# Both affine passes of the inner normalizations on VectorE, in pieces of 512 columns

## Chip, cores and metric

The kernel runs on one core of one Trainium2 chip. The metric is device time in microseconds (us) of one execution, the median of three runs. An engine here is one of the five instruction streams of the core: TensorE (PE, matmuls; PEld its weight loads), VectorE (DVE), ScalarE (ACT), GpSimd (POOL) and SyncE (SP, which issues the transfers). Each executes its own instructions in order and waits on semaphores for the others.

## What is computed

A two-layer decoder trunk on 512 tokens of width 1024. Layer 0 has a sparse attention (compressed, selected and windowed keys) beside an attention into 256 memory rows; layer 1 has a block-sparse attention beside another memory attention. Each layer ends in a gated convolutional feed-forward of width 2816. Behind each attention and each feed-forward stands a residual sum with a layer normalization, so there are four:

```python
def layer_norm(x, g, b):
    mu = xf.mean(-1, keepdims=True)
    var = jnp.square(xf - mu).mean(-1, keepdims=True)
    return (xf - mu) * lax.rsqrt(var + LN_EPS) * g + b
...
        mix = jnp.concatenate([o_main, o_mem], axis=-1) @ w_out
        x = layer_norm(ALPHA * x + mix, ln1_g[layer], ln1_b[layer])
        ffn = conv_ffn(x, ...)
        x = layer_norm(ALPHA * x + ffn, ln2_g[layer], ln2_b[layer])
```

## The kernel before

The tokens lie in four tiles of 128 rows, `nat`, each 128x1024 in float32 (in the program nat_129 or nat_2_129 is tile 0, up to nat_132 or nat_5_132 for tile 3). Every matmul of the projections is done in three products of a high and a low half (`mm3`, line 120): ScalarE copies a value to its high half (`hi`, line 114), and VectorE or GpSimd subtracts to get the low half (`lo`, line 117; for weights, line 145). Weights come in pieces of 256 KB through five buffers `raw`, always issued by SyncE.

The stream runs: layer 0 attention (heads 0 to 11), output projection, normalization (place A below), feed-forward, normalization (place B), layer 1 values, projections and attention, output projection, normalization (place C), feed-forward, and the last normalization, which writes the output. The first three are done by `norm_xT` for each tile, 12 in all: `affine` normalizes the tile in place, and `to_xT` transposes it on TensorE (line 128, 2 x 4 transposes into `psPT`, three PSUM buffers) into `xh` and `xl`, the halves that all later projections read. The last normalization is `norm_out`, with cuts of its own (`OUT_CUT`).

`affine(tb, gt, bt, cut)` does the work of one tile. `stats` takes mean and variance on VectorE (lines 521, 522). Columns below `cut` are done on VectorE: line 553 computes (x - mu) * g in one instruction, line 560 computes x * y + b in pieces of at most 512. Columns from `cut` on are done by ScalarE and GpSimd: line 549 negates the mean (VectorE), line 550 subtracts it (ScalarE), line 551 multiplies by g (GpSimd), line 562 multiplies by y (ScalarE), line 563 adds b (GpSimd). Between the two passes `rstd` (lines 529 to 537) works out y, the reciprocal deviation, on VectorE in eleven instructions on one column each, by an integer guess and two refining steps. In `norm_xT` the cut is MID_CUT = 640, so VectorE has 640 columns (a second pass of 512 + 128) and GpSimd 384.

Around A and C, `tail_heads` does the last four heads of the attention, first for tokens 0 to 255 and then for 256 to 511, with the output projection of tiles 0 and 1 between (`out_part`: lines 498, 499 split the attention result, line 505 adds the product to `nat`), then the normalization of tiles 0 and 1, then projection and normalization of tiles 2 and 3. Line 280 writes a head's sum to `o`, which the projection reads. The feed-forward behind it starts with two column blocks done for tokens 0 to 255 first (96 matmuls of 128x256), which need only tiles 0 and 1. Around B, the feed-forward's last chunks are accumulated tile by tile (line 655 adds the product to `nat`), and the memory projections and the values of layer 1 (24 matmuls of 128x256 for each tile of tokens) follow.

The order in each engine's queue isn't that of the code. The framework's scheduler places the instructions by its own estimate of times, with a high priority for what stands under `high_priority(URGENT)`, as `norm_xT` and the sums of the heads do. What an edit changes in durations can therefore move other instructions.

Of the kernel before, what the change touches and what calls it, by code (L numbers as in the profile page):

```python
# [14 lines left out]
ALU = mybir.AluOpType  # L15
# [43 lines left out]
YB = (("PT", "PT"), ("mm", "mm"), ("S", "S"), ("PT", "O"))  # L59
HALVES = ((0, 512), (512, D))  # L60
OUT_CUT = ((0, 0), (0, 0), (512, 1024), (512, 768))
MID_CUT = 640
URGENT = 1000


class Trunk:
# [115 lines left out]
        self.xh = self.al("xh", R).rearrange("p (k t) -> p k t", k=KC)  # L182
        self.xl = self.al("xl", R).rearrange("p (k t) -> p k t", k=KC)

    # ---------------------------------------------------------------- setup
    def setup(self):
        nc, a = self.nc, self.a
        self.oh = self.al("kj")
        self.rb = self.one.tile([33, NH], F, name="rb")
        nc.vector.memset(self.rb[32:33, :], -BIG)  # L190
        self.nat = [self.al("nat") for _ in range(NT)]
        x = lambda tb, c0, c1: nc.sync.dma_start(self.nat[tb][:, c0:c1], a["x"][0, tb * 128:tb * 128 + 128, c0:c1])
        x(0, 0, 512)
        x(0, 512, D)
        nc.sync.dma_start(self.rb[0:32, :], a["rel_bias"])
        nc.sync.dma_start(self.oh[0:33, 0:NREV], a["onehot"])
        self.wkv = self.al("kj")
        nc.sync.dma_start(self.wkv.rearrange("p (k m) -> p k m", k=KC),
                          a["a_w_in"][0][:, 768:896].rearrange("(k p) m -> p k m", p=128))
        for tb in range(1, NT):  # L200
            x(tb, 0, D)
        self.ident = self.one.tile([128, 128], F, name="ident")
        make_identity(nc, self.ident)
        self.i2 = self.one.tile([64, 32], F, name="i2")
        nc.vector.tensor_add(self.i2, self.ident[0:64, 0:32], self.ident[0:64, 32:64])
        self.cw = self.one.tile([128, 2, NF * 3], F, name="cw")
        self.cb = self.one.tile([128, 2, NF], F, name="cb")
        self.new_xT()
        for tb in range(NT):
            self.to_xT(tb)  # L210
# [29 lines left out]
            self.nc.sync.dma_start(t[p:p + REP, c0:512], src)  # L240
        return t

    # ---------------------------------------------------------------- pieces of attention
    def q2(self, ps, half):
        t = self.al("qq", R)
        o, e = 64 * half, 64 - 64 * half
        self.nc.scalar.activation(t[o:o + 64, :], ps[o:o + 64, :], AF.Copy, scale=SC)
        self.nc.vector.scalar_tensor_tensor(t[e:e + 64, :], ps[o:o + 64, :], SC, t[o:o + 64, :].bitcast(F),  # L248
                                            op0=ALU.mult, op1=ALU.subtract)
        return t  # L250
# [69 lines left out]
                self.mm(o, v(c), ph[:, e0:e1], start and c == 0, False)  # L320
                self.mm(o, v(c), pl[:, e0:e1], False, last)

    # ---------------------------------------------------------------- memory attention
    def mem_kv(self, w, tag="mm", rt="kj"):
        nc, a = self.nc, self.a
        t = self.al("o", R)
# [74 lines left out]
    def new_o(self):  # L401
        self.o = self.al("o").rearrange("p (k t) -> p k t", k=KC)

    # ---------------------------------------------------------------- compressed keys and values
    def stacked(self, ps, row):
        t = self.al("p")
        self.hi(t[0:64, 0:S], ps[row:row + 64, :])
        self.hi(t[64:128, 0:S - 1], ps[row:row + 64, 1:S])
        return t
# [77 lines left out]
        self.lo(pl, ps, ph)  # L487
        return ph, pl

    # ---------------------------------------------------------------- projection back, norm  # L490
    def out_part(self, w, chunks, tb, first, last):
        nc = self.nc
        n = len(chunks)
        t = self.al("kj", R)[:, 0:256 * n].rearrange("p (s k t) -> p s k t", s=2, k=n)
        for k0 in range(0, n, 2):
            c = chunks[k0]
            src = self.o[:, c:c + 2, 128 * tb:128 * tb + 128]
            self.hi(t[:, 0, k0:k0 + 2, :], src)
            self.nc.gpsimd.tensor_sub(t[:, 1, k0:k0 + 2, :], src, t[:, 0, k0:k0 + 2, :].bitcast(F))
        for half in range(2):  # L500
            sl = slice(512 * half, 512 * half + 512)
            ps = self.ps("S" if last and tb % 2 else "mm")
            for k in range(n):
                self.mm3(ps, t[:, 0, k, :], t[:, 1, k, :], w[k][0][:, sl], w[k][1][:, sl], k == 0, k == n - 1)
            nc.vector.scalar_tensor_tensor(self.nat[tb][:, sl], self.nat[tb][:, sl], ALPHA if first else 1.0, ps,  # L505
                                           op0=ALU.mult, op1=ALU.add)
            if not last and (n > 2 or half):
                yield
# [31 lines left out]
    def affine(self, tb, gt, bt, cut, cut2=None, done=None):  # L540
        nc = self.nc
        x = self.nat[tb]
        cut2 = cut if cut2 is None else cut2
        with self.tc.high_priority(URGENT):
            mu, var = self.stats(tb)
        d, p = slice(0, cut), slice(cut, D)
        if cut < D:
            nm = self.small(1)
            nc.vector.tensor_scalar(nm, mu, -1.0, None, op0=ALU.mult)
            nc.scalar.activation(x[:, p], x[:, p], AF.Identity, bias=nm)  # L550
            nc.gpsimd.tensor_mul(x[:, p], x[:, p], gt[:, p])  # L551
        if cut:
            nc.vector.scalar_tensor_tensor(x[:, d], x[:, d], mu, gt[:, d], op0=ALU.subtract, op1=ALU.mult)  # L553
        with self.tc.high_priority(URGENT):
            y = self.rstd(var)
        for c0, c1, eng in ((0, cut2, nc.vector), (cut2, D, nc.gpsimd)):
            for c in range(c0, c1, 512):
                c = slice(c, min(c + 512, c1))
                if eng is nc.vector:
                    eng.scalar_tensor_tensor(x[:, c], x[:, c], y, bt[:, c], op0=ALU.mult, op1=ALU.add)  # L560
                else:
                    nc.scalar.activation(x[:, c], x[:, c], AF.Copy, scale=y)
                    eng.tensor_add(x[:, c], x[:, c], bt[:, c])
                if done:
                    done(c)
# [5 lines left out]
    def norm_xT(self, tb, gt, bt):  # L571
        with self.tc.high_priority(URGENT):
            self.affine(tb, gt, bt, MID_CUT)
            self.to_xT(tb)

    # ---------------------------------------------------------------- feed-forward
    def ffn(self, l, last):
        nc, a = self.nc, self.a
        self.los = (nc.gpsimd,)
# [99 lines left out]
            if tb < 2:  # L679
                yield  # L680

    # ---------------------------------------------------------------- layers
    def layer0(self):
        nc, a = self.nc, self.a
        w = a["a_w_in"][0]
# [233 lines left out]
```

## Time and profile before

| | us |
|---|---|
| median of 3 runs (1282.27 to 1283.21) | 1282.38 |
| span of the profiled execution | 1278.2 |
| median less that span | 4.2 |

The profile is of one execution; its span goes from the first to the last instruction, and a time of its own from outside isn't given. Busy time is counted by engine; a matmul's end is modelled, since matmuls overlap. The granted clock is the share of TensorE's full speed of 2.4 GHz (1.00 in most stretches; 0.50 is 1.2 GHz). In square brackets stands how long an engine was idle before an instruction, and whose end it waited for.

### The profile page before, as it was taken

Reading aid. Unit: us, or ns where it says so; the run is one execution under the profiler, and the core shown is the slowest. Engines: PE = TensorE matmul, PEld = TensorE weight load, DVE = VectorE, ACT = ScalarE, POOL = GpSimd, SP = SyncE. Lnnn points to the kernel's source line nnn. Section 1 sums busy time; section 2 is a strip of 40 time slices with the busy share of each in tenths; the row PEclk is TensorE's granted clock in tenths of the full one; section 3 lists DMA queues with packets and bytes.
Section 4 is the critical chain, followed back from the end, with each engine's and each line's share of the span. In section 5 each row is a group of like instructions: output and inputs, shape, how many; then the busy total and the mean of one; then the engine's idle time right before and its main releaser. Section 6 shows DMA issues by size and latency. Waiting matters only on the chain.

```text
span 1278.2 us, 18386 instructions
## 1 busy us (share of the span) xinstructions
PE 1231.1 (96%) x6400; PEld 1048.4 (82%) x6400; DVE 726.7 (57%) x1605; ACT 596.5 (47%) x1271; POOL 275.7 (22%) x364
## 2 busy tenths in 40 slices
PE   7899999989999999999998999998999999999996
PEld 6788888879888888888888898886988888888885
DVE  5457787898544444433385665558854444443347
ACT  6457776664433333333344877465443333332232
POOL 0146443543000000000053445344400000000004
PEclk9899999999999999999999999999999999999999
DMA  9772112242433333333414223234143333333321
GB/s 230 218 201 75 42 34 58 48 127 83 120 95 99 99 99 99 98 89 95 131 42 124 67 78 89 74 100 140 35 131 99 99 92 93 97 99 99 99 74 66
DMA packets 164724, 125.94 MB, mean 99 GB/s; under 512 B 10743, under 2 KB 141175, under 8 KB 164632
## 3 DMA queue, kind: packets, MB, share of 16 engines
q1 hardware_dynamic: 164632, 124.77, 34.0%
q8 instruction: 51, 0.84, 0.3%
q14 instruction: 41, 0.34, 0.1%
HBM read 121.65 MB, written 3.08 MB: 98 GB/s over the span
## 4 chain that ended last, share of the span: by engine, by line
PE 82%; DVE 10%; DMA 3%; ACT 2%; issue 1%; POOL 0%; SPq 0%; DVEq 0%; ACTq 0%; POOLq 0%
PE psmm L120 40%; PE psS L120 27%; PE psPT L120 7%; PE psO L120 5%; PE psPT L128 3%; DVE pt L117 1%; DMA kj<-in_mem_dram 1%; DVE st L521 1%; DVE p L295 1%; DVE nat L553 1%; DVE nat L560 1%; DVE nat L505 1%; ACT p L300 1%; DVE xl L117 1%; ACT pt L114 1%
## 5 line engine op out<-in xcount | busy, mean ns | idle before, releaser
L114 ACT ACTIVATE hi<-raw 128x512 fp32r<-128x512 f32 x370 | 213.5, 622 | 274.2 <-PE psS L120 181.3
L145 DVE TENSOR_TENSOR lo<-raw,hi 128x512 fp32r<-128x512 f32 x294 | 192.0, 692 | 188.6 <-ACT hi L114 187.1
L120 PE MATMUL psmm<-xh,hi 128*128 128x512 f32 (+1 forms) x560 | 212.1, 379 | 0.0
L120 PE MATMUL psmm<-xh,lo 128*128 128x512 f32 (+1 forms) x560 | 211.9, 378 | 0.0
L120 PE MATMUL psmm<-xl,hi 128*128 128x512 f32 (+1 forms) x560 | 211.8, 378 | 0.0
L145 POOL TENSOR_TENSOR lo<-raw,hi 128x512 fp32r<-128x512 f32 x76 | 99.3, 1330 | 399.8 <-ACT hi L114 398.3
L120 PE MATMUL psS<-xh,hi 128*128 128x512 f32 (+1 forms) x408 | 151.3, 371 | 0.9 <-ACT G L750 0.9
L120 PE MATMUL psS<-xl,hi 128*128 128x512 f32 (+1 forms) x408 | 151.5, 371 | 0.1
L120 PE MATMUL psS<-xh,lo 128*128 128x512 f32 (+1 forms) x408 | 150.9, 370 | 0.0
L120 PE MATMUL psmm<-hi,kj 128*128 128x512 f32 x392 | 137.3, 400 | 4.2 <-ACT kj L114 3.2
L120 PEld LDWEIGHTS psmm<-xh,lo 128*128 128x128 f32 x560 | 105.5, 188 | 18.9
L120 PEld LDWEIGHTS psmm<-xh,hi 128*128 128x128 f32 x560 | 105.4, 188 | 18.8 <-DVE qq L248 0.2
L120 PEld LDWEIGHTS psmm<-xl,hi 128*128 128x128 f32 x560 | 105.3, 188 | 18.8
L551 POOL TENSOR_TENSOR nat<-nat,p 128x384 f32<-128x384 f32 (+2 forms) x16 | 20.5, 1283 | 360.9 <-issue 329.5
L304 POOL TENSOR_SCALAR p<-p,s 128x128 f32<-128x128 f32 (+3 forms) x144 | 74.7, 536 | 96.4 <-DVE s L271 49.1
L300 ACT ACTIVATE p<-p,s 128x128 f32<-128x128 f32 (+3 forms) x144 | 79.9, 556 | 33.0 <-DVE s L295 32.2
L120 PEld LDWEIGHTS psmm<-hi,kj 128*128 128x128 f32 x392 | 73.7, 189 | 19.4 <-ACT kj L114 3.5
L120 PEld LDWEIGHTS psS<-xh,hi 128*128 128x128 f32 x408 | 77.5, 190 | 14.0 <-ACT G L750 1.0
L120 PEld LDWEIGHTS psS<-xl,hi 128*128 128x128 f32 x408 | 77.4, 190 | 13.3 <-DVE xl L117 0.3
L120 PEld LDWEIGHTS psS<-xh,lo 128*128 128x128 f32 x408 | 77.4, 190 | 12.8
L120 PE MATMUL psPT<-hi,kj 128*128 128x512 f32 x228 | 81.7, 389 | 0.0
L295 DVE CUSTOM_DVE_ANT_0 p<-psS,T 128x128 f32<-128x128 f32 (+3 forms) x144 | 66.1, 484 | 23.1 <-PE psS L120 19.9
(269 smaller groups left out, 2235.6 us busy)
## 6 DMA issues: line engine op xcount, KB each, us to landing
raw<-in_ffn_w_in_dram SPq DMA_DIRECT2D x176, 256.0 KB, 3.1
raw<-in_ffn_w_out_dram SPq DMA_DIRECT2D x88, 256.0 KB, 3.0
T<-bias_rows SPq DMA_DIRECT2D x144, 64.0 KB, 2.0
raw<-in_shared_w_kv_dram SPq DMA_DIRECT2D x24, 256.0 KB, 3.0
raw<-in_a_w_out_dram SPq DMA_DIRECT2D x16, 256.0 KB, 2.9
raw<-in_b_w_in_dram SPq DMA_DIRECT2D x16, 256.0 KB, 3.1
raw<-in_b_w_out_dram SPq DMA_DIRECT2D x16, 256.0 KB, 3.2
raw<-in_a_w_in_dram SPq DMA_DIRECT2D x14, 256.0 KB, 3.9
```

What stands on the lines that cost most here:

```text
L114: self.nc.scalar.activation(dst, src, AF.Copy)
L117: self.nc.vector.tensor_sub(dst, src, hi.bitcast(F))
L120: self.nc.tensor.matmul(o, l, r, start=start, stop=stop)
L128: self.nc.tensor.transpose(o, i, self.ident)
L145: eng.tensor_sub(l[:, c], raw, h[:, c].bitcast(F))
L295: nc.vector.tensor_tensor_reduce(L[i], dst[i], T[:, 384 - 128 * i:512], op0=ALU.add, op1=ALU.min, scale=1.0, scalar=BIG, accum_out=nm[:, i ...
L300: nc.scalar.activation(L[i], L[i], AF.Exp, bias=nm[:, i:i + 1], scale=-1.0, accum_out=sm[:, i:i + 1])
L304: nc.gpsimd.tensor_scalar(L[i], L[i], r[:, i - qs[0]:i - qs[0] + 1], 1.0, op0=ALU.mult, op1=ALU.mult)
L505: nc.vector.scalar_tensor_tensor(self.nat[tb][:, sl], self.nat[tb][:, sl], ALPHA if first else 1.0, ps, op0=ALU.mult, op1=ALU.add)
L521: nc.vector.bn_stats(st[:, 6 * j:6 * j + 6], x[:, c0:c1])
L551: nc.gpsimd.tensor_mul(x[:, p], x[:, p], gt[:, p])
L553: nc.vector.scalar_tensor_tensor(x[:, d], x[:, d], mu, gt[:, d], op0=ALU.subtract, op1=ALU.mult)
```

## The change

MID_CUT becomes 1024, so `norm_xT` gives all 1024 columns to VectorE and lines 549 to 551, 562 and 563 aren't reached for these twelve tiles. The first pass on VectorE, one instruction so far, is done in pieces of 512, as the second was. The last normalization has cuts of its own and keeps its instructions (its VectorE part of 512 columns is one piece).

```diff
-MID_CUT = 640
+MID_CUT = 1024
...
         if cut:
-            nc.vector.scalar_tensor_tensor(x[:, d], x[:, d], mu, gt[:, d], op0=ALU.subtract, op1=ALU.mult)
+            for c in range(0, cut, 512):
+                c = slice(c, min(c + 512, cut))
+                nc.vector.scalar_tensor_tensor(x[:, c], x[:, c], mu, gt[:, c], op0=ALU.subtract, op1=ALU.mult)
```

In the built program the scheduler moves other instructions too, at A, B and C; the transfers keep their order. In the changed kernel the first pass is line 555 and the second line 562. Two places follow.

VectorE's queue in place A, before, around the sum of the last head (line 280, into `o`) and tile 1's second pass (line 560):

```order
L537 SCALAR_TENSOR_TENSOR s4_800_3745<-s4_801_3746,s4_800_3745 128x1
L117 TENSOR_TENSOR xl_782_3655<-psPT_795_3721,xh_781_3654 128x4x128
L560 SCALAR_TENSOR_TENSOR nat_3_130<-nat_3_130,s4_800_3745,p_772_3631 128x512
L560 SCALAR_TENSOR_TENSOR nat_3_130<-nat_3_130,s4_800_3745,p_772_3631 128x128
L280 TENSOR_TENSOR o_67_542<-psO_742_3517,ot_767_3608 64x256
```

The same place in the changed kernel:

```order
L562 SCALAR_TENSOR_TENSOR nat_2_129<-nat_2_129,s4_791_3701,p_772_3631 128x512 x2
L534 SCALAR_TENSOR_TENSOR s4_799_3738<-s4_799_3738 128x1
L280 TENSOR_TENSOR o_67_542<-psO_742_3517,ot_767_3608 64x256
L535 SCALAR_TENSOR_TENSOR s4_798_3737<-s4_799_3738,s4_798_3737 128x1
L536 SCALAR_TENSOR_TENSOR s4_799_3738<-s4_798_3737,s4_800_3739 128x1
L117 TENSOR_TENSOR xl_782_3655<-psPT_794_3716,xh_781_3654 128x4x128
L537 SCALAR_TENSOR_TENSOR s4_798_3737<-s4_799_3738,s4_798_3737 128x1
L562 SCALAR_TENSOR_TENSOR nat_3_130<-nat_3_130,s4_798_3737,p_772_3631 128x512 x2
```

The head's sum now stands between tile 0's second pass and tile 1's, no longer behind both.

TensorE's queue in place B, before, around the transposes of tile 3 (nat_5_132, line 128); psmm_1267 and psmm_1268 are the value projections of the first two tiles of tokens:

```order
L120 MATMUL psmm_1267_6886<-lo_1264_6877,xh_1086_5683 128x256
L120 MATMUL psmm_1267_6886<-hi_1263_6876,xl_1087_5684 128x256
L128 MATMUL psPT_1255_6850<-ident_142,nat_5_132 128x128 x4
L128 MATMUL psPT_1256_6857<-ident_142,nat_5_132 128x128
L120 MATMUL psmm_1268_6913<-hi_1259_6866,xh_1086_5683 128x256
L120 MATMUL psmm_1268_6913<-lo_1260_6867,xh_1086_5683 128x256
```

The same place in the changed kernel, where these projections are psmm_1259 and psmm_1260, and that of the third tile psmm_1261:

```order
L120 MATMUL psmm_1260_6873<-hi_1255_6836,xh_1082_5663 128x256
L120 MATMUL psmm_1260_6873<-lo_1256_6837,xh_1082_5663 128x256
L128 MATMUL psPT_1247_6810<-ident_142,nat_5_132 128x128 x4
L120 MATMUL psmm_1260_6873<-hi_1255_6836,xl_1083_5664 128x256
L128 MATMUL psPT_1248_6817<-ident_142,nat_5_132 128x128 x4
L120 MATMUL psmm_1261_6900<-hi_1251_6826,xh_1082_5663 128x256
```

The transposes of tile 3 moved behind 23 of the 24 matmuls of the second tile's projection, and the first four are no longer followed by one that reads columns 512 to 639.

## Rows read from the trace of the kernel before

**Rows 1.** The page: the span, and busy time of each engine with its share

```profile
span 1278.2 us, 18386 instructions
PE 1231.1 (96%) x6400; PEld 1048.4 (82%) x6400; DVE 726.7 (57%) x1605; ACT 596.5 (47%) x1271; POOL 275.7 (22%) x364
```

**Rows 2.** Windows: stretch, length, busy PE, PEld, DVE, ACT, POOL, clock, DMA share, GB/s

```profile
275.00:290.00 15.00, 10.81 (x74) 8.38 (x73) 14.77 (x47) 9.15 (x19) 7.31 (x9) 1.00 0.51 157
...
682.00:688.00 6.00, 6.00 (x39) 5.87 (x38) 1.48 (x4) 0.98 (x2) 0.59 (x1) 0.72 0.16 46
...
895.00:902.00 7.00, 6.75 (x21) 5.47 (x22) 5.66 (x11) 2.22 (x5) 3.87 (x4) 0.59 0.00 0
```

**Rows 3.** Groups by line and shape, 270 to 930 us: count, busy, mean ns

```profile
L553 DVE SCALAR_TENSOR_TENSOR nat<-nat,s,p 128x640 f32<-128x640 f32 x12 | 12.4, 1030 | 0.0
...
L560 DVE SCALAR_TENSOR_TENSOR nat<-nat,s,p 128x512 f32<-128x512 f32 x12 | 9.0, 746 | 0.2
...
L560 DVE SCALAR_TENSOR_TENSOR nat<-nat,s,p 128x128 f32<-128x128 f32 x12 | 6.9, 573 | 0.0
...
L534 DVE SCALAR_TENSOR_TENSOR s<-s 128x1 f32<-128x1 f32 x12 | 8.5, 707 | 0.1
...
L537 DVE SCALAR_TENSOR_TENSOR s<-s,s 128x1 f32<-128x1 f32 x12 | 1.9, 157 | 0.2
```

**Rows 4.** Timeline of place A, VectorE: start, duration, what (tile 1; tiles 2 and 3)

```profile
285.93 0.14 DVE L535 SCALAR_TENSOR_TENSOR s<-s,s 128x1 f32<-128x1 f32 x1
...
287.04 1.75 DVE L560 SCALAR_TENSOR_TENSOR nat<-nat,s,p 128x512 f32<-128x512 f32 x2
288.82 0.42 DVE L280 TENSOR_TENSOR o<-psO,ot 64x256 f32<-64x256 f32 x1
...
296.96 1.83 DVE L553 SCALAR_TENSOR_TENSOR nat<-nat,s,p 128x640 f32<-128x640 f32 x1
...
306.77 1.02 DVE L560 SCALAR_TENSOR_TENSOR nat<-nat,s,p 128x512 f32<-128x512 f32 x2
```

**Rows 5.** Timeline of place A, TensorE: projection of tile 2, feed-forward's second half

```profile
289.74 0.50 PE L120 MATMUL psmm<-hi,kj 128*128 128x512 f32 x1 [0.18 <-ACT kj L114]
...
309.90 0.39 PE L120 MATMUL psS<-xl,hi 128*128 128x256 f32 x1
```

**Rows 6.** Timeline of place A, GpSimd: weight subtractions, the last sum

```profile
295.54 5.65 POOL L145 TENSOR_TENSOR lo<-raw,hi 128x512 fp32r<-128x512 f32 x4 [4.25 <-ACT hi L114]
...
307.52 1.13 POOL L563 TENSOR_TENSOR nat<-nat,p 128x384 f32<-128x384 f32 x1 [1.45 <-ACT nat L562]
```

**Rows 7.** Timeline of place B, TensorE: end of a value projection, tile 3's transposes

```profile
677.37 0.28 PE L120 MATMUL psmm<-lo,xh 128*128 128x256 f32 x1
677.49 0.28 PE L120 MATMUL psmm<-hi,xl 128*128 128x256 f32 x1
681.49 0.77 PE L128 MATMUL psPT<-ident,nat 128*128 128x128 f32 x5 [3.73 <-DVE nat L560]
```

**Rows 8.** Timeline of place B, VectorE: tile 3's sum, third refining step, second pass

```profile
671.30 0.67 DVE L655 SCALAR_TENSOR_TENSOR nat<-nat,psO 128x512 f32<-128x512 f32 x1
...
677.16 1.23 DVE L535 SCALAR_TENSOR_TENSOR s<-s,s 128x1 f32<-128x1 f32 x1
...
680.68 1.01 DVE L560 SCALAR_TENSOR_TENSOR nat<-nat,s,p 128x512 f32<-128x512 f32 x2
```

**Rows 9.** Timeline of place C, TensorE: the two waits

```profile
891.11 1.16 PE L120 MATMUL psO<-pt,v 128*128 128x256 f32 x8 [2.04 <-DVE o L280]
895.25 0.80 PE L120 MATMUL psmm<-hi,kj 128*128 128x512 f32 x1 [2.99 <-ACT kj L114]
```

**Rows 10.** Timeline of place C, VectorE: tile 1's first pass, the last head's sum

```profile
892.49 0.87 DVE L553 SCALAR_TENSOR_TENSOR nat<-nat,s,p 128x640 f32<-128x640 f32 x1
893.29 0.94 DVE L536 SCALAR_TENSOR_TENSOR s<-s,s 128x1 f32<-128x1 f32 x1
...
894.33 0.42 DVE L280 TENSOR_TENSOR o<-psO,ot 64x256 f32<-64x256 f32 x1
```

## Prediction

> **What bounds the kernel now.** I read the page first: of a span of 1278.2 us TensorE is busy 96%, VectorE 57%, GpSimd 22% [rows 1]. A TensorE-bound kernel gains from this change only where TensorE waits for a normalization or runs at half clock because it waited. So the next view is the windows around the three places where normalizations stand inside the program: A, after the first attention (275 to 310 us), B, after the first feed-forward (638 to 694), C, after the second attention (886 to 920). In A's first 15 us TensorE is busy 10.81 us and VectorE 14.77: VectorE is the limit there. Behind B's wait and behind C's two waits the granted clock is 0.72 over 6 us and 0.59 over 7 us, which are stretches at 1.2 GHz mixed with 2.4 [rows 2]. Everything else is TensorE at full clock, and nothing of the change touches it.
>
> **What the edit costs each engine.** Per token tile (12 of them) two ScalarE passes and two GpSimd products and sums of 384 columns go (the last GpSimd sum in A takes 1.13 us [rows 6]), with one 128x1 VectorE instruction, which I leave out. VectorE takes their columns. Its first pass of 640 columns takes 0.87 us undisturbed [rows 10], a pass of 512 takes 0.75 [rows 3], so 128 columns are worth 0.12 us, and the pair 512+128 takes 1.02 [rows 4]. A pair 512+512 is then 1.02 + 3 x 0.12 = 1.38 us. First pass: 1.38 - 0.87 = +0.51; second: 1.38 - 1.02 = +0.36; together +0.87 us of VectorE per tile, 3.5 us per place, 10.4 us in all.
>
> Against that stands time in which VectorE waits for GpSimd. The 640 pass averages 1.03 us instead of 0.87, the 128-column piece 0.57 where the pair above leaves 0.27, and the one-column instruction of L534 0.71 where that of L537 takes 0.16 [rows 3]: 12 x (0.16 + 0.30 + 0.55) = 12.1 us, and L535 and L536 can be as long (1.23 at 677.16, 0.94 at 893.29 [rows 8, 10]), so I estimate up to 20 us blocked in all. The pair at 287.04 took 1.75 us instead of 1.02, the pass at 296.96 took 1.83, with the GpSimd subtractions from 295.54 on beside it [rows 4, 6]. Some of these stand beside the removed GpSimd work and some beside the weight subtractions that stay; I credit half, 10 us, with 0 and 20 as bounds. VectorE's sum then comes out at nought (10.4 added, 10 given back). The gain has to come from order, and from the chain behind the last tile.
>
> The Trainium skill, SBUF — State Buffer, section Who interferes with whom, says that a VectorE instruction with two SBUF inputs and a GpSimd instruction that reads SBUF exclude each other for a whole instruction. The rows at 296.96 and 287.04 agree. It speaks against the change as much as for it, since the new pieces have two SBUF inputs too and the weight subtractions (L145) stay on GpSimd; what that would do is the second rival.
>
> **Place A.** Now the last head's sum (L280) stands in VectorE's queue behind tile 1's second pass: that pass starts at 287.04, L280 at 288.82, and TensorE's output projection for tiles 2 and 3 at 289.74 [rows 4, 5]. In the changed order L280 stands ahead of tile 1's second pass, and TensorE does the projection ahead of tile 1's transposes. What it passes stands now from L535 at 285.93 to 288.82 [rows 4], 2.9 us; ahead of that, three longer passes (+1.4 us) and the waits on L551 and L563 that go (an estimated 1.5) about cancel. So L280 starts near 286, and the projection, which waits for nothing else, 2.9 us earlier. The work put off (three small instructions, one copy, the pass of tile 1) lies beside 24 projection matmuls of 0.23 us, 5.5 us. At the far end the feed-forward's second half starts at 309.90 [rows 5]; before it stands the 96-matmul first half, 11.5 us, and it is this, no longer the chain of tile 3 (second pass 306.77, then ScalarE, then GpSimd from 307.52 [rows 4, 6]), that ends last: the GpSimd step goes, worth 1.1 us. I take -2.6 us for A. Bounds: -4.2 (all idle time of 275 to 290) and +1.0 (VectorE's 3.5 us with half of the blocked time left).
>
> **Place B.** Here TensorE's order decides. Tile 3's transposes stand right behind the value projection of tokens 0 to 127, whose last matmul starts at 677.49; they start at 681.49, after 3.73 us of waiting [rows 7], and the clock of the next 6 us is 0.72, so 6 x 0.28 = 1.7 us more are lost [rows 2]. Together 5.4 us. In the changed order 23 of the 24 matmuls of tokens 128 to 255 stand ahead of these transposes: 23 x 0.12 (677.37 to 677.49 [rows 7]) = 2.8 us of cover, to 680.4. The transposes then also need only the first 512 columns of the second pass. Even with VectorE no earlier, that piece is done at 680.68 + 0.69 = 681.4 [rows 8], so the wait falls from 3.73 to about 1 us. And VectorE should be earlier: tile 3's sum (671.30 [rows 8]) stood behind two subtractions and, in the new order, is due near 669.3, as the ScalarE copies that these wait for come sooner; behind it stand +0.5 us for the first pass and waits of up to 1.2 us each on GpSimd's subtractions (L535 at 677.16 [rows 8]). I expect the first piece between 677 and 682.9, most likely 679, thus no wait and no fall of the clock; waits under 1 us in A left it at 1.00 [rows 2]. B: -5.4 us, bounds -5.6 and -1.5 (2.5 us of wait and the clock down again).
>
> **Place C.** TensorE waits 2.04 us for the sum of a head before the last and 2.99 us for the last head's [rows 9]. The first moves later by 0.5 us, the longer pass being in front of it; the second (L280 at 894.33 [rows 10]) gets 2 x 0.5 more in front and loses the 0.7 us for which L536 was blocked by L551, so it moves by +0.1 to +0.3. The waits together stay near 5 us, so the half clock stays. At the end, the feed-forward's second half is released as in A, and the GpSimd step goes there: 1.1 as in A at most, and -0.8 as I take it, since a copy on VectorE comes next. C: -0.6, bounds -3.5 (the clock does not fall: 7 x 0.41 = 2.9 more) and +1.5.
>
> **Sum.** -2.6 - 5.4 - 0.6 = -8.6 us on a profiled span of 1278.2. The median of the runs, 1282.4, is 4.2 us above that span, and I carry this over: 1282.4 - 8.6 = 1273.8. Behind the places the feed-forwards and the second attention run as TensorE allows, so earlier starts should be kept.
>
> **Rivals.**
> 1. The wait in B shrinks but something takes its place (VectorE held up by GpSimd's subtractions in tile 3's chain, or weights not yet split when TensorE arrives), and A or C gives nothing: B -3 to -4, A and C between -1 and +1: 1277.4 to 1279.8. For it: L535 of that chain was blocked for 1.1 us [rows 8]. Against: the order alone covers 2.8 us.
> 2. Slower: VectorE is the bound of A and C, and the blocked time does not go with L551 and L563 but passes to the subtractions that remain. Then A and C each get +3.5 us, and in B 3.73 + 3.5 - 2.8 = 4.4 us of wait leave +0.7 and the half clock: +7.7, 1290. It decides from the point where less than 0.87 us per tile is given back. For it: VectorE is busy 14.77 of 15 us in A. Against: in A's first half and in most of C GpSimd has little else to do than the removed work.
> 3. No change: the earlier starts are given back later, by weight loads or by the buffers in front of the feed-forward. 1280 to 1285. For it: every load shares one queue. Against: no load is in the last waits of A, B or C.
> That the edit is not done is ruled out by the order of the built program: no GpSimd or ScalarE pass is left in the twelve tiles.
>
> **How the numbers follow.** Forecast (1269.5 to 1277.4) 0.62; rival 1 0.13; rival 3 0.12; rival 2 0.13. Faster by over 0.2% (about what a measurement of this kernel can tell from no change), below 1279.8: 0.62 + 0.13 = 0.75; within 0.12; slower 0.13. The range goes from 1269.5 (A and B at their best ends, 1282.4 - 4.2 - 5.6 = 1272.6, less 3 of C's clock) to 1281.5, which takes in rival 1 and a part of rival 3, and leaves out about 0.2.
>
> **What would show it.** A: L280 of the last head near 286 and the output projection within 1 us behind it; wrong if the projection starts after 289. B: the idle time ahead of tile 3's transposes under 1 us and the clock 1.00 in the 6 us behind; wrong if it exceeds 2. C: two waits of together about 5 us, and a clock near 0.6 behind them. VectorE's busy time over the span within 3 us of 726.7. The forecast fails most easily if GpSimd's remaining subtractions hold VectorE longer than they did.

## The result, and the profile after

The changed kernel took 1275.67 us (median of four runs, 1274.09 to 1277.62) against 1282.8 for the kernel before beside it: a ratio of 0.9944, 95% interval 0.9928 to 0.996. Timed again in the last experiments, on one chip with more runs, the ratio is 0.9959 (0.9945 to 0.9974), that is 5.3 us (3.3 to 7.1). The forecast was faster by 8.6 us, to 1273.8, with a range from 1269.5 to 1281.5: the sign was right and the time is in the range. What the three places gave is another matter, and most of this part is about it.

The page of the changed kernel, against [rows 1]:

```profile
span 1273.5 us, 18311 instructions
...
PE 1227.6 (96%) x6400; PEld 1045.3 (82%) x6400; DVE 728.1 (57%) x1605; ACT 582.9 (46%) x1247; POOL 247.7 (19%) x340
```

GpSimd lost 28 us, ScalarE 13.6, and VectorE, which took over all of it, gained 1.4. The groups by line and shape, 270 to 930 us (count, busy, mean ns), show why, against [rows 3]; line 555 is the first pass now and 562 the second, and from there on the changed kernel's lines are two higher than before's. Lines 533 to 537 are the five refining steps, half of the ten one-column instructions that `rstd` has (three of them are line 529; eleven, as said above, is one too many):

```profile
L555 DVE SCALAR_TENSOR_TENSOR nat<-nat,s,p 128x512 f32<-128x512 f32 x24 | 20.1, 874 | 0.0
L562 DVE SCALAR_TENSOR_TENSOR nat<-nat,s,p 128x512 f32<-128x512 f32 x24 | 17.9, 784 | 0.2
...
L536 DVE SCALAR_TENSOR_TENSOR s<-s,s 128x1 f32<-128x1 f32 x12 | 4.1, 338 | 0.2
L534 DVE SCALAR_TENSOR_TENSOR s<-s 128x1 f32<-128x1 f32 x12 | 3.4, 286 | 0.1
L533 DVE SCALAR_TENSOR_TENSOR s<-s,s 128x1 f32<-128x1 f32 x12 | 3.4, 281 | 0.1
L535 DVE SCALAR_TENSOR_TENSOR s<-s,s 128x1 f32<-128x1 f32 x12 | 3.2, 271 | 0.1
L537 DVE SCALAR_TENSOR_TENSOR s<-s,s 128x1 f32<-128x1 f32 x12 | 3.1, 261 | 0.2
```

The same groups before, for the three steps that [rows 3] leaves out:

```profile
L536 DVE SCALAR_TENSOR_TENSOR s<-s,s 128x1 f32<-128x1 f32 x12 | 5.6, 464 | 0.2
L535 DVE SCALAR_TENSOR_TENSOR s<-s,s 128x1 f32<-128x1 f32 x12 | 5.4, 454 | 0.2
L533 DVE SCALAR_TENSOR_TENSOR s<-s,s 128x1 f32<-128x1 f32 x12 | 3.6, 302 | 0.1
```

The passes rose from 28.3 to 38.0 us, and the five one-column refining steps fell from 25.0 to 17.2. So of the 9.7 us that the passes cost, 7.8 came back as time in which VectorE no longer stands still beside GpSimd, and 1.8 with line 549, which is gone.

**A ledger by place.** The runs of one kernel differ by some 3 us, but not where the change is. I use four marks on VectorE, the same instruction in every trace: M1, the first statistics of place A (line 521, 266.57 before); M2, a gating product inside the first feed-forward (line 593, 350.11); M3, the first query subtraction behind place B (line 248, 700.16); M4, a gating product inside the second feed-forward (959.93). M1 to M2 holds place A, M2 to M3 place B, M3 to M4 place C, and from M4 to the end every kernel takes the same 318.2 us (317.7 in e5 and e6, whose edit reaches the last normalization too). M1 itself lies anywhere from 265.8 to 269.3 in the twelve traces of this study, whatever the kernel: that is where the runs differ. It is not the change that differs there: ahead of M1 TensorE, VectorE, ScalarE and GpSimd execute the same instructions in the same order in all these kernels, except that e4 has four subtractions fewer on GpSimd. Part of the difference is TensorE's clock: from 68 to 71 and from 225 to 228 us it is 0.50 in the trace of before and 1.00 in the first trace of the change (M1 at 265.94), and in the second trace of the change it is 0.50 and 0.78 (M1 at 268.56). In us, less than before:

| kernel | A | B | C | ratio of the times |
|---|---|---|---|---|
| before, traced again (e0) | -0.04 | -0.02 | +0.03 | 0.9998 (0.9987 to 1.0008) |
| the change | -1.89 | -2.15 | -0.04 | 0.9944 (0.9928 to 0.996) |
| the change, again (e8) | -1.88 | -2.18 | +0.38 | 0.9959 (0.9945 to 0.9974) |
| at B alone (e1) | -0.08 | -2.17 | -0.29 | 0.9968 (0.9955 to 0.9981) |
| at A and C alone (e2) | -1.90 | -0.31 | -0.05 | 0.9996 (0.9984 to 1.0009) |
| before, transposes late in B (e3) | +0.01 | +1.07 | -0.13 | 1.0005 (0.9992 to 1.0017) |
| the change, GpSimd's subtractions out (e4) | -1.88 | -4.25 | +1.33 | one run |
| the change, one-operand steps (e5) | +1.22 | -1.01 | +1.01 | 0.9986 (0.9972 to 1.0) |
| before, one-operand steps (e6) | -2.39 | -3.33 | -0.78 | 0.9946 (0.9926 to 0.9965) |
| the change, first pass in one piece (e7) | -2.36 | -2.07 | -1.04 | 0.9952 (0.9935 to 0.9969) |
| e7, one-operand steps in two tiles of B (e9) | -2.38 | -4.27 | -0.87 | 0.9942 (0.9925 to 0.996) |

The two kernels that were traced twice agree with themselves within 0.05 us at A and B and within 0.5 at C. At C that half a microsecond goes with the clock: over 7 us from the end of the second wait it is 0.67 in the first trace of the change and 0.57 in the second. So the change gives 1.9 us in A, 2.15 in B and nothing in C: 4.1 us, half of what I summed.

**Place A**, VectorE, against [rows 4] (start, duration, what):

```profile
285.33 0.42 DVE L280 TENSOR_TENSOR o<-psO,ot 64x256 f32<-64x256 f32 x1
...
287.09 1.85 DVE L562 SCALAR_TENSOR_TENSOR nat<-nat,s,p 128x512 f32<-128x512 f32 x2
...
295.21 3.40 DVE L555 SCALAR_TENSOR_TENSOR nat<-nat,s,p 128x512 f32<-128x512 f32 x2
...
304.12 1.42 DVE L562 SCALAR_TENSOR_TENSOR nat<-nat,s,p 128x512 f32<-128x512 f32 x2
```

and TensorE, against [rows 5], with GpSimd's row against [rows 6]:

```profile
286.27 0.50 PE L120 MATMUL psmm<-hi,kj 128*128 128x512 f32 x1 [0.27 <-ACT kj L114]
...
290.04 0.60 PE L128 MATMUL psPT<-ident,nat 128*128 128x128 f32 x4
...
292.10 0.60 PE L128 MATMUL psPT<-ident,nat 128*128 128x128 f32 x4
...
307.39 0.39 PE L120 MATMUL psS<-xl,hi 128*128 128x256 f32 x1
```

```profile
292.55 5.51 POOL L145 TENSOR_TENSOR lo<-raw,hi 128x512 fp32r<-128x512 f32 x4 [4.82 <-ACT hi L114]
```

The head's sum and the projection come 3.5 us earlier than before, of which 0.63 was there at M1 already. But from the projection to the feed-forward's second half it is 21.12 us now and was 20.16: tile 1's eight transposes, which before stood in front of the projection, stand inside it (290.04 and 292.10).

**Place B**, TensorE, against [rows 7], and VectorE, against [rows 8]:

```profile
665.21 0.66 PE L128 MATMUL psPT<-ident,nat 128*128 128x128 f32 x4 [0.48 <-DVE nat L562]
...
668.16 0.35 PE L120 MATMUL psmm<-hi,o 128*128 128x256 f32 x1 [1.10 <-DVE kj L117]
...
678.43 0.36 PE L120 MATMUL psmm<-hi,xh 128*128 128x256 f32 x1 [1.41 <-DVE kj L117]
...
681.26 0.60 PE L128 MATMUL psPT<-ident,nat 128*128 128x128 f32 x4
```

```profile
659.39 1.23 DVE L534 SCALAR_TENSOR_TENSOR s<-s 128x1 f32<-128x1 f32 x1
...
663.15 1.21 DVE L537 SCALAR_TENSOR_TENSOR s<-s,s 128x1 f32<-128x1 f32 x1
...
675.54 0.99 DVE L535 SCALAR_TENSOR_TENSOR s<-s,s 128x1 f32<-128x1 f32 x1
676.56 1.19 DVE L536 SCALAR_TENSOR_TENSOR s<-s,s 128x1 f32<-128x1 f32 x1
...
677.87 0.42 DVE L117 TENSOR_TENSOR kj<-psmm,kj 128x256 fp32r<-128x256 f32 x1
678.20 1.40 DVE L562 SCALAR_TENSOR_TENSOR nat<-nat,s,p 128x512 f32<-128x512 f32 x2
```

GpSimd in the same stretch:

```profile
656.80 7.55 POOL L145 TENSOR_TENSOR lo<-raw,hi 128x512 fp32r<-128x512 f32 x6 [24.20 <-ACT hi L114]
...
675.22 2.52 POOL L145 TENSOR_TENSOR lo<-raw,hi 128x512 fp32r<-128x512 f32 x2 [2.93 <-ACT hi L114]
```

Tile 3's transposes (681.26) don't wait any more. Three other waits have come, 0.48, 1.10 and 1.41 us, that before has not. The last one is not for the normalization at all: the value projection of the second tile waits for a subtraction (line 117, `kj` out of `psmm`; the expectations call it a copy) that empties its PSUM buffer, and this one stands on VectorE behind lines 535 and 536, which take 0.99 and 1.19 us beside GpSimd's two subtractions.

**Place C**, TensorE, against [rows 9], and the windows that answer to [rows 2] (stretch, length, busy PE, PEld, DVE, ACT, POOL, clock, DMA share, GB/s):

```profile
886.87 1.15 PE L120 MATMUL psO<-pt,v 128*128 128x256 f32 x8 [2.51 <-DVE o L280]
890.75 0.80 PE L120 MATMUL psmm<-hi,kj 128*128 128x512 f32 x1 [2.73 <-ACT kj L114]
```

```profile
274.40:289.40 15.00, 12.08 (x78) 9.74 (x77) 14.80 (x47) 6.60 (x15) 3.94 (x6) 1.00 0.52 157
677.50:683.50 6.00, 5.07 (x43) 5.10 (x44) 3.38 (x9) 1.36 (x3) 0.24 (x1) 1.00 0.32 92
890.50:897.50 7.00, 6.75 (x25) 5.48 (x26) 5.91 (x12) 1.10 (x3) 2.17 (x2) 0.67 0.00 0
```

C's two waits add up to 5.24 us, and the half clock behind them is still there; in B the clock holds at 1.00. At C's far end, the last four transposes of the place wait as they did, first before, then in the changed kernel:

```profile
918.53 0.66 PE L128 MATMUL psPT<-ident,nat 128*128 128x128 f32 x4 [0.38 <-DVE xl L117]
```

```profile
913.82 0.66 PE L128 MATMUL psPT<-ident,nat 128*128 128x128 f32 x4 [0.41 <-DVE xl L117]
```

### The profile page after: what moved, and what is told of

Same layout as the page of the kernel before. It is cut to its first block, busy times and chain, and to the rows that moved or that the text cites. A ratio compares the mean times of both kernels' runs of the same rounds, so it can differ in the third digit from the quotient of the medians.

```text
span 1273.5 us, 18311 instructions
## 1 busy us (share of the span) xinstructions
PE 1227.6 (96%) x6400; PEld 1045.3 (82%) x6400; DVE 728.1 (57%) x1605; ACT 582.9 (46%) x1247; POOL 247.7 (19%) x340
## 4 chain that ended last, share of the span: by engine, by line
PE 83%; DVE 9%; DMA 3%; ACT 2%; issue 1%; POOL 0%; SPq 0%; DVEq 0%; ACTq 0%; POOLq 0%
PE psmm L120 40%; PE psS L120 28%; PE psPT L120 7%; PE psO L120 5%; PE psPT L128 3%; DVE pt L117 1%; DVE p L295 1%; DMA kj<-in_mem_dram 1%; DVE nat L555 1%; ACT p L300 1%; DVE nat L562 1%; DVE xl L117 1%; ACT pt L114 1%; DVE nat L505 1%; DVE st L521 1%
## 5 line engine op out<-in xcount | busy, mean ns | idle before, releaser
L120 PEld LDWEIGHTS psS<-xh,hi 128*128 128x128 f32 x408 | 77.4, 190 | 13.9 <-ACT G L752 1.2
L117 DVE TENSOR_TENSOR pt<-psPT,pt 128x512 fp32r<-128x512 f32 (+2 forms) x124 | 73.5, 605 | 7.5 <-ACT pt L114 6.7
```

Of the source, the lines that this page charges most:

```text
L117: self.nc.vector.tensor_sub(dst, src, hi.bitcast(F))
L120: self.nc.tensor.matmul(o, l, r, start=start, stop=stop)
```

## Experiments

### First, the places apart

**e0, the kernel before again.** No edit.

> The kernel before, unchanged, as a control. The trace of before has a span of 1278.2 us and the changed kernel's trace 1273.5, 4.7 less, while the medians of the runs differ by 7.1 (1282.8 and 1275.7). Theory (the trace of before was a fast draw): this kernel's runs have spans between 1279 and 1283, each 1.8 us below its time, and its profile reaches the sums of the heads and the feed-forwards within 0.5 us of the same distances as the trace of before, so that the difference lies ahead of place A. Rival (something in the changed kernel outside the three places gives 2.4 us): spans near 1278 with times near 1282, the distance between the two staying at 4.2.

Its spans lie between 1277.2 and 1281.4 (four of the ten under the 1279 that I had expected), each 1.88 to 1.97 us below its own time, and the trace agrees with that of before within 0.05 us at all three places. So the trace of before was one of the faster executions (M1 at 266.57; here at 268.55), and the rival is out: the distance of 4.2 us between span and time was not the kernel's.

**e1 and e2, the change at some places only.** The cut is chosen by the place of the call:

```diff
-MID_CUT = 1024
+CUTS = (640, 1024, 640)
...
     def norm_xT(self, tb, gt, bt):
+        cut = CUTS[self.nnorm // NT]
+        self.nnorm += 1
         with self.tc.high_priority(URGENT):
-            self.affine(tb, gt, bt, MID_CUT)
+            self.affine(tb, gt, bt, cut)
```

In e2 it is (1024, 640, 1024), and a cut of 640 is one piece, as before.

> The change at place B alone (after the first feed-forward), A and C as before. Theory (the places are independent, each worth what its own stretch of the traces shows): A and C gain nothing (within 0.3 us), B gains 2.1 us, as in the changed kernel, where the first 2 us of the gain are lost again between 660 and 680 us; the median is 2 us under before. Rival 1 (A's earlier arrival at B collides with the weights, so that B alone gives what was forecast): B gains 5 us or more. Rival 2 (B's gain needs A's): B gains under 1 us.

> The change at places A and C, B as before. Theory: A gains 1.9 us (2.5 at the start of the feed-forward's second half less 0.6 that was there ahead of A), C nothing (within 0.3), and B's wait of 3.73 us and its half clock are back, so the span is about 2 us under that of before. Rival (the gain in the medians, 7.1, belongs to A's stretch): 4 us or more.

B alone gives 2.17 us, A and C alone 1.90 and 0.05: the places are independent, and each gives alone what it gives in the whole, within the 0.3 us by which the places without the change move too. By the times e1 is 4.1 us under before (2.4 to 5.8) and e2 0.5 (2.1 under to 1.2 over): these intervals are as wide as what they are to tell. The ledger's sum is 2.5 for e1, just inside its interval, and 2.3 for e2, just outside. The ledger separates the places, the times don't.

### Place B: order, or a held VectorE?

**e3, the order alone.** The kernel before, with tile 3's transposes tied behind the second tile's value projection on TensorE; every engine keeps its work.

```diff
-            self.to_xT(tb)
+            if not late:
+                self.to_xT(tb)
...
-        for _ in values(0):
-            pass
+        for tb, _ in enumerate(values(0)):
+            if tb == 1:
+                with self.tc.issue_after(self.last_mm.ins):
+                    self.to_xT(3)
```

> The kernel before with the order of TensorE in place B alone: the transposes of tile 3 stand behind all 24 matmuls of the second tile's value projection, everything else (the split over VectorE, ScalarE and GpSimd, 640 columns) as it was. The prediction took these matmuls as cover that is ready: if they are, the wait falls from 3.73 us to about 1 and the clock stays at 1.00, so B gains 4 to 5 us. The rival, from the trace of the changed kernel: there these matmuls waited 1.41 us for a copy of VectorE (line 117, kj out of psmm) that stood behind the third refining step; in before that copy stands at 680.16, behind line 536, so the matmuls would start at about 680.6, the wait only falls from 3.73 to 3, the half clock stays or is shortened, and B gains 0.5 to 1.5 us.

Both were wrong, and my forecast's step by far the more. TensorE's and VectorE's rows, and the window behind the wait:

```profile
684.63 0.55 PE L120 MATMUL psmm<-hi,xh 128*128 128x256 f32 x1 [4.56 <-DVE kj L117]
```

```profile
682.61 0.42 DVE L117 TENSOR_TENSOR kj<-psmm,kj 128x256 fp32r<-128x256 f32 x1
...
684.07 0.42 DVE L117 TENSOR_TENSOR kj<-psmm,kj 128x256 fp32r<-128x256 f32 x1
```

```profile
682.00:688.00 6.00, 3.37 (x16) 3.40 (x17) 2.75 (x7) 1.16 (x3) 1.56 (x2) 0.50 0.46 134
```

The projection that was to cover the wait waits itself, 4.56 us, until the second of the two subtractions of line 117, at 684.07, which stands behind the first pieces of tile 3's second pass; the clock goes to half, and B loses 1.07 us. The order is no cover: the matmuls and the transposes wait for the same queue of VectorE. What the change gained in B it gained on VectorE; whether it needed the new order as well no run shows, and e6 below gains more there with the transposes of tile 3 where they were before.

**e4, GpSimd's weight subtractions left out** in A, B and C (the high half is read for the low one):

```diff
         eng = self.los[self.nlo % len(self.los)]
+        cut = self.skip and eng is self.nc.gpsimd
+        if cut:
+            l = h
...
-            eng.tensor_sub(l[:, c], raw, h[:, c].bitcast(F))
+            if not cut:
+                eng.tensor_sub(l[:, c], raw, h[:, c].bitcast(F))
```

> The changed kernel with the weight subtractions (L145) that fall on GpSimd beside the normalizations in A, B and C left out: these weights' high half is read in place of their low half, so the result is another one, at the same number of matmuls. Theory (in B VectorE's one-column refining steps L533 to L537 are held by GpSimd's subtractions, 4.9 us instead of 0.9 for tile 2 and 2.8 instead of 0.9 for tile 3, and TensorE's waits of 0.48, 1.10 and 1.41 us come from that): the five one-column steps take about 0.15 to 0.25 us each everywhere, the three waits go, and B gains 5 us against before instead of 2.15; in A the pair of pieces that took 3.40 us takes 1.4, and A gains 1 to 2 us more than 1.9. Rival (VectorE simply has too much of its own work in these stretches): the waits stay within 0.3 us, B gains 2 to 2.6.

B gains 4.25 instead of 2.15. The waits of 0.48 and 1.10 us are gone. That of 1.41 is there with 1.40, and its row tells why: the two subtractions beside it belong to a weight that the edit didn't reach (GpSimd's row is the last).

```profile
678.95 0.36 PE L120 MATMUL psmm<-hi,xh 128*128 128x256 f32 x1 [1.40 <-DVE kj L117]
```

```profile
677.09 1.19 DVE L540 SCALAR_TENSOR_TENSOR s<-s,s 128x1 f32<-128x1 f32 x1
...
678.39 0.42 DVE L117 TENSOR_TENSOR kj<-psmm,kj 128x256 fp32r<-128x256 f32 x1
```

```profile
675.74 2.52 POOL L149 TENSOR_TENSOR lo<-raw,hi 128x512 fp32r<-128x512 f32 x2 [3.27 <-issue]
```

(Lines are four higher here: L540 is line 536.) In A the pair of 3.40 us takes 1.41 now, as expected, but A stays at 1.88, which I had expected to rise by 1 to 2 us: A's end is not VectorE's chain but TensorE's own work ahead of the last transposes, where it waits 0.41 us here and 0.43 in the changed kernel. C lost 1.3 us at a wait in the last heads of its attention, ahead of its normalizations: 1.89 us for GpSimd at 875.41, with the clock at 0.50 from 876.3 to 879.5. Why GpSimd came late there is open.

### The refining steps with one tensor operand

If it is the second tensor operand through which GpSimd holds VectorE, the five steps of `rstd` can be had without one, since their second operand is one column and so can be a per-partition scalar:

```diff
-        nc.vector.scalar_tensor_tensor(t, y, v[:, 1:2], y, op0=ALU.mult, op1=ALU.mult)
+        nc.vector.tensor_scalar(t, y, v[:, 1:2], y, op0=ALU.mult, op1=ALU.mult)
...
-        nc.vector.scalar_tensor_tensor(y, t, 1.875, y, op0=ALU.add, op1=ALU.mult)
+        nc.vector.tensor_scalar(y, t, 1.875, y, op0=ALU.add, op1=ALU.mult)
```

**e6, this in the kernel before**, with GpSimd's passes as they were:

> The kernel before with the refining steps written with one tensor operand, as in the run on the changed kernel. Theory: the one-column steps of tile 3 in B (0.87 + 1.23 + 1.21 us) shrink by up to 2.8 us, part of which the 640-column pass or the 512-column piece pays back beside the same subtractions; TensorE's wait of 3.73 us falls to 1 to 2.5 and B gains 1.5 to 4 us without any change of the two passes; the sum of the five steps falls from 25 us to about 10. Rival (the wait is set by something else): 3.73 stays within 0.5 us.

Groups of e6, 262 to 930 us, and TensorE's wait in B:

```profile
L560 DVE SCALAR_TENSOR_TENSOR nat<-nat,s,p 128x128 f32<-128x128 f32 x12 | 9.9, 825 | 0.0
...
L536 DVE TENSOR_SCALAR s<-s,s 128x1 f32<-128x1 f32 x12 | 3.2, 268 | 0.2
...
L534 DVE TENSOR_SCALAR s<-s 128x1 f32<-128x1 f32 x12 | 2.5, 208 | 0.1
```

```profile
677.45 0.76 PE L128 MATMUL psPT<-ident,nat 128*128 128x128 f32 x5 [2.22 <-DVE nat L560]
```

The five steps take 13.9 us in all instead of 25.0, each of the sixty 0.19 to 0.28 us whether GpSimd works beside it or not, so none of them was held. The Trainium skill, SBUF — State Buffer, section Who interferes with whom, says that a VectorE instruction with at most one SBUF input, and not in one of the modes that use both ports, doesn't contend with GpSimd; the rows agree, and show that here per-partition scalars didn't count as inputs. Part of the held time passes on to the next instruction with two: the 128-column piece rose from 573 to 825 ns [rows 3]. Enough is left that TensorE's wait falls to 2.22 us, the clock stays at 1.00, and five edited lines give 6.5 us at the three places, more than the 4.1 of the whole change; the intervals of the times don't part the two. Only B's share can be put down to the steps: there 1.5 us less of wait and 1.7 of clock make 3.2 of the 3.33, and tile 3's transposes kept their place. In A the scheduler gave this kernel the change's order too: the head's sum (286.05) stands ahead of tile 1's second pass (287.54), and tile 1's eight transposes stand inside the projection or right behind it. A gains 2.4 us so with GpSimd's passes still there; no run parts the new order from the cheaper steps.

**e5, the same edit in the changed kernel:**

> The changed kernel with the five one-column refining steps (L533 to L537) written as instructions with one tensor operand and two per-partition scalars, instead of two tensor operands; the arithmetic is the same. If it is the second tensor operand that lets GpSimd hold a VectorE instruction (the one-operand steps L529 to L531 take 0.14 us at all times in both traces), the five steps take 0.15 to 0.2 us each, some 10 us in all 12 tiles instead of 17.2, and B gains 1 to 3 us more than 2.15, the part that is not passed on to the 512-column pieces behind them. Rival (any VectorE instruction is held, or the scalars count as operands too): the sums stay near 17 us and B at 2.15 within 0.5.

The steps fell to 13.8 us here too, and the kernel became slower than the changed one by 3.1 us in A, 1.1 in B and 1.0 in C. The scheduler placed the cheaper form otherwise. TensorE's waits in B and A:

```profile
673.39 0.65 PE L128 MATMUL psPT<-ident,nat 128*128 128x128 f32 x4 [2.76 <-DVE s L531]
```

```profile
296.58 0.39 PE L120 MATMUL psS<-xh,hi 128*128 128x256 f32 x1 [1.20 <-ACT xh L114]
```

Behind the wait in A the clock fell to 0.50 for 3.4 us, an estimated 1.7 us more, which is over the wait itself:

```profile
299.00:302.00 3.00, 3.00 (x16) 3.00 (x16) 2.93 (x10) 0.00 (x0) 0.99 (x1) 0.50 0.64 188
```

In B tile 2's second pass had gone behind tile 3's first pass and two weight subtractions, and its transposes came late by 2.76 us. So the expectation on the steps held and that on B failed, for a reason that neither theory had: an edit that shortens instructions is an edit of the order too.

**e7, the first pass of the change in one instruction of 1024 columns:**

```diff
-            for c in range(0, cut, 512):
-                c = slice(c, min(c + 512, cut))
+            for c in (0,):
+                c = slice(0, cut)
```

> The changed kernel with the first pass as one instruction of 1024 columns instead of two of 512. By the prices of the traces a pair 512+512 takes 1.40 us and 640 columns 0.87, so that 1024 columns take about 1.3: 0.1 us less per tile. Theory (the pieces don't matter for the first pass, since nothing reads it before the second): every place within 0.4 us of the changed kernel. Rival (the cut lets GpSimd's subtractions in between the pieces, or the other way about): a difference of over 1 us in A, where the pair took 3.40 us beside the subtractions.

A gains 0.5 us more than with the pieces, C 1.0 to 1.4, B nothing (-2.07). The second wait in C is shorter (1.78 us; 2.73 in the first trace of the change and 1.91 in the second):

```profile
892.28 0.79 PE L120 MATMUL psmm<-hi,kj 128*128 128x512 f32 x1 [1.78 <-ACT kj L114]
```

Most of what C gains is not this wait but the clock, 0.76 from 892 to 899 us, where the change has 0.67 and 0.57 over the same stretch: 7 us x 0.09 is an estimated 0.6 of the 1.0 against the first trace. The theory's 0.4 us was too narrow for A and C, and the rival's difference of over 1 us in A didn't come. That the cut lets GpSimd in is not shown; the scheduler's order differs in A and C as well.

**e9, e7 with the one-operand steps in B's tiles 2 and 3 alone**, where TensorE's order stays that of e7 but for tile 2's two groups of four transposes, which move by two matmuls and by one, and one matmul in C:

```diff
+        step = nc.vector.tensor_scalar if self.nnorm in (6, 7) else nc.vector.scalar_tensor_tensor
+        self.nnorm += 1
-        nc.vector.scalar_tensor_tensor(t, y, v[:, 1:2], y, op0=ALU.mult, op1=ALU.mult)
+        step(t, y, v[:, 1:2], y, op0=ALU.mult, op1=ALU.mult)
```

> The changed kernel with the first pass in one piece, as run before, and the five one-column refining steps with one tensor operand in place B's tiles 2 and 3 alone; by the order of the built program the transposes of tile 2 move by three matmuls and nothing else moves on TensorE. Theory (TensorE's waits in B of 0.47, 1.15 and 1.48 us come from these steps being held by GpSimd, and what is held instead costs less): the steps take 0.2 to 0.27 us each, the waits together fall from 3.1 us to under 1.5, B gains 3.5 to 5 us against before instead of 2.07, A and C stay at 2.4 and 0.8 within 0.3, and the kernel is 6.5 to 8 us under before. Rival (held time only passes on to the next two-operand instruction, the second pass or the weights' subtractions on VectorE, and reaches TensorE all the same): the waits stay at 2.5 us or more and B at 2 to 2.6.

B gains 4.27 us, as the theory had it. Of e7's waits of 0.47, 1.15 and 1.48 us the first and the last are gone, and 1.23 stand where 1.15 stood. Why that one stayed is on VectorE and GpSimd (lines are one to three higher: L565 is the second pass, L146 line 145):

```profile
666.91 0.36 PE L121 MATMUL psmm<-hi,o 128*128 128x256 f32 x1 [1.23 <-DVE kj L118]
```

```profile
660.55 2.92 DVE L565 SCALAR_TENSOR_TENSOR nat<-nat,s,p 128x512 f32<-128x512 f32 x2
663.39 1.78 DVE L146 TENSOR_TENSOR lo<-raw,hi 128x512 fp32r<-128x512 f32 x1
```

```profile
656.16 8.46 POOL L146 TENSOR_TENSOR lo<-raw,hi 128x512 fp32r<-128x512 f32 x6 [24.24 <-ACT hi L115]
```

The held time has passed to the second pass (2.92 us instead of 1.41) and a weight subtraction (1.78 instead of 0.68), and those stand ahead of the subtraction of line 118 that TensorE waits for. This is the best kernel of the study by the places, 7.5 us under before. By the times it is 0.9942, which the intervals don't part from the change's.

**e8, the change again**, beside e9:

> The changed kernel, unchanged, timed again beside before on one chip. Theory (the places give 1.9 us in A, 2.15 in B and nothing in C, each reproduced within 0.2 us by a second trace, and what the medians showed beyond these 4.1 us was the spread of the runs ahead of place A): the places come out the same in this trace within 0.3 us, and the medians lie 3.5 to 5.5 us apart. Rival (the medians' 7.1 us is what the change is worth, and some of it lies where the two traces don't show it): 6.5 us or more.

A and B as in the first trace, C 0.4 higher, which is more than the theory's 0.3; the medians lie 6.0 apart, between what the theory and the rival wanted, and 5.3 us by the ratio. The theory stands for A and B. The interval (3.3 to 7.1) doesn't exclude the rival's 6.5 or more; the ledger does for everything behind M1, where the gain is 3.7 us in this trace, and ahead of M1 both kernels execute the same.

## Why the forecast was right, and where its steps failed

**The price on VectorE** was right. A pair of pieces takes 1.41 us undisturbed, so the passes cost (1.41 - 0.87) + (1.41 - 1.02) = 0.93 us per tile against 0.87 forecast. The blocked time given back is 7.8 us in the refining steps (25.0 - 17.2) and 1.4 in the passes: these were held for 28.3 - 12 x (0.87 + 1.02) = 5.6 us before and for 38.0 - 24 pairs of pieces x 1.41 = 4.2 after. That is 9.2 against my 10. VectorE's sum is 728.1, within 3 of 726.7. The L280 row and the waits in C came out as said, too.

**Place A**, -2.6 forecast, -1.9 measured. The first half was right: the head's sum at 285.33 (forecast near 286), the projection within 1 us. The term that was missing is TensorE's own: the transposes of tile 1 that are put off from ahead of the projection into it. I had listed three small instructions, one copy and a pass as "the work put off", all of them off TensorE, and not the eight transposes; with them the stretch to the feed-forward's second half is 0.96 us longer, and the 2.9 us by which the projection was to come earlier (2.84 behind M1) became 1.9. A second term had no wait behind it: 1.1 us for the GpSimd step at the far end. There TensorE waited 0.32 us before, for VectorE's line 560, and waits 0.43 now, for VectorE's line 117, which empties the transposes' buffer. How 2.9 and 1.1 make 2.6 the prediction doesn't say. The second half came 2.51 us earlier than in the trace of before, as the forecast's 2.6 wanted, but 0.63 of it was that execution's head start at M1.

**Place B**, -5.4 forecast, -2.15 measured. What was aimed at came true: no wait at tile 3's transposes, first piece at 678.20 (forecast 677 to 682.9, most likely 679), the clock at 1.00. Two steps failed. First, the cover: "23 of the 24 matmuls of tokens 128 to 255 stand ahead of these transposes: ... 2.8 us of cover" took these matmuls as ready, and they wait for a PSUM buffer that VectorE empties behind the same refining steps; e3 shows that this order alone makes it worse. Second, the stretch ahead of it: I costed tile 3's chain and not tile 2's, whose steps GpSimd's six subtractions in a row held from 658 to 664; this gave two waits (0.48 and 1.10). These five steps were held before too, without a wait on TensorE, and took 3.1 us; in the change they take 4.9. So for this tile the blocked time was not given back but grew, as rival 2 had it: from M2 to tile 2's second pass it was 314.5 us and is 316.8. With these three waits 5.4 - 3.0 = 2.4, against 2.15. The cause of all three is what I had named for rival 1, VectorE held by GpSimd's subtractions in B; that they come from it is shown for the first two by e4, and for the first again and the last by e9.

**Place C**, -0.6 forecast, between 0 and +0.4 measured: the waits as forecast (5.24 against "near 5"), the clock too (0.67 and, in the second trace, 0.57); the 0.8 for the GpSimd step at its end didn't come. TensorE's only wait there is 0.38 us before and 0.41 after, both times put down to VectorE's line 117, which ended as late as GpSimd's last sum did (918.5), so there was next to nothing for the step's going to give. In A e4 shows besides that a shorter chain at the end gives nothing.

**The sum**, -8.6, is twice what the places give (4.1). That 1273.8 lies within 2 us of the measured median is partly the draw: the medians of the first four runs differ by 7.1, those of the larger comparison by 6.0, its ratio gives 5.3. The 4.2 us that I carried over as median less span are 1.9 of a fixed distance and 2.3 by which that one execution was faster than the median. One reading was wrong without harm to the sum: "Everything else is TensorE at full clock". The trace of before is at half clock near its start, from 68 to 71 and from 225 to 228 us and at its end as well; ahead of A this comes and goes from one execution to the next. Rival 2 fell as a whole, though its mechanism is there in tile 2 of B and in the pair of 3.40 us in A: VectorE is busy 14.80 of 15 us in A, and A is still faster. Rival 3 fell: from M2 to the end of the first feed-forward, and from M4 to the end, nothing is given back.

## What to carry to other kernels

A block of matmuls covers a wait only if its operands and its PSUM buffer come from elsewhere: look up who empties the buffer that it writes, and where that instruction stands in its queue, before it is counted as ready. Where two engines hold each other, ask which instruction form is held before work is moved from one to the other; rewriting five one-column steps in the form that isn't held gave more in B than moving both passes (3.3 us against 2.15), though in the changed kernel the same lines lost 5.3 us at the three places, by the order that came of them. And cost every instruction that a new order moves, those of the bounding engine first.

## What was not expected of the hardware

- The five refining steps, one column each, take 0.14 to 0.22 us alone and up to 1.23 us beside GpSimd's 1.3 us subtractions with two tensor operands, and 0.16 to 0.28 at all times with one tensor operand and scalars (e5, e6). A subtraction with one operand in PSUM and one in SBUF (line 117, 0.68 us) kept its time beside the same GpSimd subtractions.
- Two pieces of 512 columns took 1.41, 1.85, 2.44, 2.92 and 3.40 us in these traces, by what GpSimd did beside them.
- TensorE's clock after waits in B: 3.73 us were followed by 0.72 over 6 us [rows 2, 7], 4.56 by 0.50, 2.76 (e5) by 0.86 from 676 to 682; after 2.22 (e6) and after 1.41 it stayed at 1.00. But 1.89 us in the last heads of C (e4) were followed by 0.50 over 3 us, and so were 1.20 and 0.51 us in A (e5): in these traces the length of the single wait doesn't tell whether the clock falls.
